# Reading the moving columns of four down-projections in other orders

## The chip, the core and the metric

The kernel runs on one core of a Trainium2 chip. The metric is the device time of one execution in microseconds; the time before is 997.28 us, the median of two runs. The engines are TensorE (PE, with its weight loads shown apart as PEld), VectorE (DVE), ScalarE (ACT), GpSimd (POOL) and SyncE (SP), which issues the DMAs. TensorE multiplies a stationary operand of 128 x 128 weights with a moving operand of up to 512 columns and adds the product into a bank of PSUM, its accumulator memory.

## The reference

The program is a decoder trunk of two layers over 256 tokens with 1024 features. Each layer is a half-step SwiGLU feed-forward network, a token mixer (stick-breaking attention in layer 0, a gated linear recurrence in layer 1), and another half-step feed-forward network. Each sub-layer normalises its input and is modulated by a conditioning vector. What matters here is the feed-forward network, of which there are four:

```python
def swiglu(h, w_gu, w_down):
    g, u = jnp.split(h @ w_gu, 2, axis=-1)
    return (jax.nn.silu(g) * u) @ w_down
...
    x = x + MACARON_W * g * swiglu(h, ffn_w_gu[layer, 0], ffn_w_down[layer, 0])
```

`w_down` has 2816 rows and 1024 columns. The product with it is the down-projection; its result is scaled by a gate and added to x.

## The kernel before

All activations lie with features on the 128 partitions and the 256 tokens along the columns. x is eight tiles of 128 x 256 (`xall`, lines 436 and 437), and the hidden layer of a feed-forward network is 22 such tiles. Sub-layers are named by a pair: (0,0), (0,2), (1,0) and (1,2) are the four feed-forward networks, (0,1) the attention, (1,1) the recurrence.

Every float32 number is split into a high part and a remainder, both kept as `float32r`, which TensorE takes in one pass. A product is then three matmuls into the same columns of a bank: high by high, high by remainder, remainder by high. `Acc.group` (lines 514 to 532) issues these three, all at line 526; `o`, `wc` and `xc` are functions that cut the columns of the bank, of the weights and of the moving operand:

```python
                seq = ((wh, xh), (wh, xl), (wl, xh))
                for n, i in enumerate(passes):
                    u, v = seq[i]
                    pe.matmul(o(b()), wc(u()), xc(v()), ...
```

Products with few uses are left whole and take TensorE's own float32 passes (`group32`, line 538, with its matmul at line 543: two k tiles of the recurrence's output projection, 16 matmuls). The attention's product of weights and values (line 951) and its running sums (lines 929 and 931) also call the matmul directly. In `values` the last three of each six matmuls read their moving operand as two runs of 128 columns, 384 apart, and write two runs of 128 columns, 256 apart.

`down` (from line 643) does a down-projection. The eight output tiles d lie in five banks, two to a bank but for the last two; bank halves are taken by `place`. For each k tile of the hidden layer and each d, `step(d, k)` calls `group` with the 256 columns of the hidden tile as moving operand and 256 consecutive columns of the bank as output. All but the last two chunks of weights run in the order of k; the last four k tiles run by d, so that the first output tiles are done early. Then `residual(d)` adds gate times bank to x[d] in one DVE instruction (line 666), and ACT and DVE make from x[d] the square for the next norm (`add_square`, line 601 for the sum) and the scaled tile that the next sub-layer's first products take before its norm is known (`scaled`, line 626). After the last sub-layer a sum of squares, a reciprocal root and six multiplications (line 1124) with their output DMAs end the program.

Weights arrive by DMA in pieces of 2048 columns, and `load` (from line 482) splits them on ACT (line 497) and DVE (line 500). Rows of the modulation weights are multiplied on DVE (line 564) between feed-forward tiles.

The order of all instructions is set in advance by a list scheduler (`Program.schedule`) from prices for each operation. `V(fn, T, ...)` gives a DVE operation its price by its number of columns, whatever instructions `fn` then issues, and a matmul group has a price by its columns alone. Each engine runs its own list in order, and waits for others on semaphores.

Of the kernel before, what the change touches and what calls it, by code (L numbers as in the profile page):

```python
# [44 lines left out]
NPAR = OFF_LAM + NR  # L45
NP0 = OFF_MB + 3 * KD  # what the first sub-layer needs

# [12 lines left out]

# [1 line left out]
class Space:  # L62
    """Memory that buffers take turns in, in program order: equal slots or an arena of cells."""

# [41 lines left out]
class Program:  # L106
# [58 lines left out]
    def schedule(self):  # L165
        ops = self.ops
        for o in ops:
            for d, data in o.deps.items():
                d.succ.append((o, data))
        # a buffer's users hold up whoever needs its place next  # L170
        spaces = {b.space for o in ops for b in o.bufs if b.space is not None}
# [33 lines left out]
        busy, gap, loads = 0.0, None, self.loads  # L205
        late = 0.0  # how far TensorE is behind its own time
        queue = {e: sorted((o for o in ops if o.eng == e), key=lambda o: (o.prio, o.seq)) for e in ("ACT", "DVE")}
# [4 lines left out]
        def guess(o, depth):  # L212
            """when an operation might start, from its inputs alone"""
            t = 0.0
            for d, data in o.deps.items():
                if d.start is not None:
                    t = max(t, d.end + self.lag(d, o, data))
                elif depth == 0:
                    return None
                else:  # L220
                    g = guess(d, depth - 1)
                    if g is None:
                        return None
                    t = max(t, max(g, free[d.eng]) + d.cost + self.lag(d, o, data))
            return t

        def wait_for(e, t, o):
            """an urgent operation, soon ready, that a start of o at t would hold up"""
            q = queue[e]
            while head[e] < len(q) and q[head[e]].start is not None:  # L230
                head[e] += 1
            n, i = 0, head[e]
            slack = o.prio + late - t
            while n < LOOK and i < len(q):
                u = q[i]
                i += 1
                if u.start is not None:
                    continue
                n += 1
                if u is o or u.prio >= o.prio:  # L240
                    break
                g = guess(u, 3)
                if g is None or g >= t + o.cost or g <= t:
                    continue
                if u.prio + late - g < o.cost and u.prio + late - g < slack - MARGIN:
                    return g
            return None
# [17 lines left out]
        while len(order) < len(ops):  # L265
# [60 lines left out]
            for b in o.bufs:  # L326
                b.uses -= 1
                if b.uses == 0 and b.space is not None:
                    sp = b.space
                    sp.live -= 1  # L330
                    # in-order engines: earlier readers on other engines have ended by their own time
                    t = o.end + 120.0 if b.hist else o.end
                    b.rel = max(getattr(b, "rel", 0.0), t)
                    for i in range(b.at, b.at + b.n):
                        sp.free[i] = b.rel
                    sp.last = max(sp.last, b.rel)
                else:
                    b.rel = max(getattr(b, "rel", 0.0), o.end + 120.0)
# [26 lines left out]
def trunk(ctx, tc, xT, cb, par, modw, gu0, gu, wdn, qk, wv, wo, win, wri, wout, out):  # L365
# [10 lines left out]

# [1 line left out]
    def ring(name, n, cols, dt=F32, pl=const):  # L378
# [52 lines left out]

# [1 line left out]
    def fixed(name, cols, dt=F32):  # L433
# [35 lines left out]

# [1 line left out]
    def dma(dst, src, n, w, after=(), lat=None):  # L471
# [10 lines left out]
    def load(src, n, name, chain=None, size=HALF):  # L482
        """n columns of weights: returns pieces of size columns, each (hi, lo)."""
        raw = Buf(rawr, name=f"raw_{name}")
# [22 lines left out]
    class Acc:  # L507
        """regions of one PSUM bank, with one start flag for the bank"""

# [4 lines left out]
        def group(self, part, o, w, wc, xs, xc, stop, parts=(None,), passes=(0, 1, 2)):  # L514
            """o += w[:, wc].T @ xs[:, xc] in three exact products"""
            b = self.b
# [21 lines left out]
    def group32(acc, part, o, w, wc, x32, xc, n, stop):  # L538
        """the same product, by TensorE's own float32 passes"""
        b = acc.b  # L540
# [8 lines left out]

# [1 line left out]
    mraw, mfin = {}, {}  # L551

    def mod_tile(l, s, w, t, after=(), lat=None):
        """row tile t of mod_w[l] for sub-layer s, part w (0 shift, 1 scale, 2 gate)."""
        key = (l, s, w)
# [12 lines left out]
    def mod_final(l, s, w, t0=0, n=KD):  # L568
# [4 lines left out]
        pp = [(pars, 0)] if l == s == 0 else [pars]  # L573
        mi = lambda: m()[:, t0 : t0 + n]  # noqa: E731
        fo = lambda: f()[:, t0 : t0 + n]  # noqa: E731
        if w == 0:
# [9 lines left out]

# [1 line left out]
    ssq, hcur, gcur = {}, {}, {}  # L588
# [27 lines left out]
    def scaled(gen, d):  # L616
        """x * scale and, in two more columns, the shift: what the first tile works on before the norm is known"""
        gs, sh = mfin[gen + (1,)], mfin[gen + (0,)]
        hi, lo = Buf(hxr), Buf(hxr)
        gcur.setdefault(gen, []).append((hi, lo))  # L620
        c = slice(d, d + 1)
        shc = lambda: sh()[:, c].to_broadcast([P, 2])  # noqa: E731
        A(lambda: hi()[:, T:], shc, AF.Copy, 2, [(sh, d)], [(hi, 1)])
# [19 lines left out]
    def down(l, s, nxt, srcs, ys, nlast, hook=None, post=None, n32=0):  # L643
        """x += gate * (W.T y) and what the next norm needs; srcs: chunks of two k tiles [P, 2, D];
        ys(k): (hi, lo), or one float32 tile for the first n32 chunks, and its columns."""
        accs = [Acc(f"acc_{l}_{s}_{i}") for i in range(5)]
# [5 lines left out]
        def step(d, k):  # L652
            acc, j = place[d]
            y, yc = ys(k)
            o = lambda b: b[:, j * T : (j + 1) * T]  # noqa: E731
            if k < 2 * n32:
                c0 = (k % 2) * D + d * P
                group32(acc, j, o, ws[k], lambda u: u[:, c0 : c0 + P], y, lambda v: v[:, yc], T, False)
            else:
                group(acc, j, o, ws[k], lambda u: u[:, d * P : (d + 1) * P], y, lambda v: v[:, yc], T, k == 2 * n - 1)  # L660

        def residual(d):
            acc, j = place[d]

            def fn():
                dve.scalar_tensor_tensor(x[d](), acc.b()[:, j * T : (j + 1) * T], gate()[:, d : d + 1], x[d](), ALU.mult,  # L666
                                         ALU.add)
            V(fn, T, [(acc.b, j), (gate, d), x[d]], [x[d]], ptr=1)
# [28 lines left out]
    def up(acc, ws, hx_):  # L697
        """acc = two regions of T columns: pieces of w [k, 2 P] against h"""
        for k in range(KD):
# [5 lines left out]
    def up_first(gen, ws, scale=(1.0, 1.0)):  # L705
        """the same products for the first tiles, on x * scale and shift: for each tile and region
        (tile, normed), column to add, its dependency"""
        gx = gcur.pop(gen)
# [20 lines left out]

# [1 line left out]
    def swiglu_tile(acc, y):  # L731
# [73 lines left out]

# [1 line left out]
    def attention(l, s, nxt, hook):  # L807
        R, F = new_phase(88, 24)
        # softplus(-lambda) for the recurrent block, with the same tables
        A(lam, lambda: col(OFF_LAM, NR), AF.Abs, NR, [pars], [lam], after=[pr.last_pe])  # L810
# [68 lines left out]

        W2 = 2 * S  # for each of two heads: block 0 (t = 0..255), block 1 (t = 128..255)  # L880
        BL = (slice(0, T), slice(T, S))
# [7 lines left out]
        def scores(f):  # L889
            """rows are keys s, columns queries t"""  # L890
            qh, ql = qs.pop(f)
# [49 lines left out]
        def values(f):  # L941
# [13 lines left out]
            for e in range(2):  # L955
                rows = slice(e * 64, (e + 1) * 64)
                bi = lambda e=e, rows=rows: b()[rows, e * T : (e + 1) * T]  # noqa: E731
                A(lambda rows=rows: oh()[rows, :], bi, AF.Copy, T, [b], [(oh, e)], psum=True)
# [29 lines left out]

# [1 line left out]
    def rglru(l, s, nxt):  # L990
        N32 = 1  # chunks of w_out that float32 passes take
        R, F = new_phase(8 * (NB - N32), 86)
# [137 lines left out]

# [1 line left out]
    last = []  # L1132
# [73 lines left out]

# [1 line left out]
    order = pr.schedule()  # L1208
# [58 lines left out]
```

## Time and profile before

| | |
|---|---|
| Runs | 997.07 and 997.49 us, median 997.28 |
| Profiled execution | span 994.6 us from the first to the last instruction; no time of its own is listed |
| Time outside the span | 2.7 us, from the median |
| TensorE | 980.2 us busy, 8096 matmuls |
| VectorE | 798.5 us busy |
| ScalarE | 561.8 us busy |
| DMA | 251.24 MB, 253 GB/s on average |

The span is the stretch from the first to the last instruction of one profiled execution. The page cuts it in 40 slices and shows each engine's busy share in tenths, and the clock that TensorE was granted. A line of the groups gives the kernel's line, the engine, the operation, out<-in, the shape and the count, then the busy time in us and the mean of one in ns, and then the idle time of the engine before them with what ended it. A line of the chain gives the start and the length in us of a piece of the chain of work that ended last, and how many instructions it has. The ends of matmuls are modelled, so the duration of one, some 280 ns, says little; the distance from one start to the next is what counts.

### The profile page before, as it was taken

The page shows a single profiled execution, that of the slowest core. Times are in us where ns is not written, and L with a number is a line of the kernel's source. Part 1 is how long each engine was busy: PE and PEld are TensorE (multiplying, and loading weights), DVE is VectorE, ACT ScalarE, POOL GpSimd, SP SyncE. Part 2 cuts the span into 40 slices and gives each one's busy share as a digit, 9 for nine tenths or more (in the row PEclk, how much of TensorE's full clock was granted, in tenths as well). Part 3 has the DMA queues.
Part 4 walks back from the last instruction along what each step waited for, and adds up shares of the span by engine and source line. Part 5 has one row for each costly group of instructions (what it writes and reads, how often), then busy time and mean ns, then how long its engine had stood idle before and what let it go on. Part 6 is the DMA issues. An engine that isn't in the chain of part 4 may idle for free.

```text
span 994.6 us, 19696 instructions
## 1 busy us (share of the span) xinstructions
PE 980.2 (99%) x8096; PEld 969.1 (97%) x8096; DVE 798.5 (80%) x1316; ACT 561.8 (56%) x902; POOL 2.2 (0%) x14
## 2 busy tenths in 40 slices
PE   7999999999999999999999999999999999999997
PEld 5999999999999999999999999999999999999996
DVE  7997887898988999888789989874997996555433
ACT  5475443379776854444366544443779785444333
POOL 0000000000000000000000000000000000000000
PEclk9999999999999999999999999999999999999999
DMA  9988898845666389899866988886334645545421
GB/s 341 358 317 316 326 331 304 338 166 193 241 232 234 143 307 334 328 343 336 313 266 254 333 326 334 335 308 214 107 134 163 254 176 210 205 174 191 165 111 43
DMA packets 48331, 251.24 MB, mean 253 GB/s; under 512 B 5489, under 2 KB 6129, under 8 KB 28530
## 3 DMA queue, kind: packets, MB, share of 16 engines
q1 hardware_dynamic: 48242, 249.99, 68.0%
q8 instruction: 63, 1.03, 0.4%
q14 instruction: 26, 0.21, 0.1%
HBM read 248.92 MB, written 1.05 MB: 251 GB/s over the span
## 4 chain that ended last, share of the span: by engine, by line
PE 98%; DVE 1%; DMA 0%; issue 0%; ACT 0%; SPq 0%; DVEq 0%
PE bank L526 90%; PE bank L836 2%; PE bank L902 1%; PE bank L1025 1%; PE bank L951 1%; PE bank L543 1%; PE bank L929 1%; DMA x<-in_xT 0%; PE bank L905 0%; PE bank L608 0%; PE bank L931 0%; DVE x L1124 0%; DVE ssq L1151 0%; DVE rawm L564 0%; DVEq L1262 0%
## 5 line engine op out<-in xcount | busy, mean ns | idle before, releaser
L526 PE MATMUL bank<-hx,wh 128*128 128x256 f32 (+1 forms) x3392 | 606.9, 282 | 2.5 <-ACT hx L476 2.5
L497 ACT ACTIVATE wh<-raw 128x1024 fp32r<-128x1024 f32 (+1 forms) x328 | 337.2, 1046 | 339.2 <-PE bank L526 238.3
L526 PEld LDWEIGHTS bank<-hx,wh 128*128 128x128 f32 x3392 | 520.7, 189 | 4.1 <-ACT hx L476 3.3
L500 DVE TENSOR_TENSOR wl<-raw,wh 128x1024 fp32r<-128x1024 f32 (+1 forms) x328 | 390.1, 1209 | 129.4 <-ACT wh L497 126.0
L526 PE MATMUL bank<-hx,wl 128*128 128x256 f32 (+1 forms) x1696 | 475.3, 280 | 0.0
L526 PEld LDWEIGHTS bank<-hx,wl 128*128 128x128 f32 x1696 | 320.5, 189 | 0.0
L526 PE MATMUL bank<-arenar,wh 128*128 128x256 f32 x1664 | 294.7, 280 | 0.0
L526 PEld LDWEIGHTS bank<-arenar,wh 128*128 128x128 f32 x1664 | 254.1, 188 | 0.1
L526 PE MATMUL bank<-arenar,wl 128*128 128x256 f32 x832 | 232.4, 279 | 0.0
L564 DVE SCALAR_TENSOR_TENSOR rawm<-rawm,cact 128x1024 f32<-128x1024 f32 x144 | 174.8, 1219 | 19.7 <-DMA rawm<-in_modw 19.3
L526 PEld LDWEIGHTS bank<-arenar,wl 128*128 128x128 f32 x832 | 156.1, 188 | 0.0
L476 ACT ACTIVATE arenar<-a 128x256 fp32r<-128x256 f32 x88 | 35.3, 404 | 4.4 <-DVE a L735 4.4
L740 DVE TENSOR_TENSOR arenar<-a,arenar 128x256 fp32r<-128x256 f32 x88 | 36.4, 418 | 0.5 <-ACT arenar L476 0.5
L735 DVE TENSOR_TENSOR a<-bank,sg 128x256 f32<-128x256 f32 x82 | 34.1, 418 | 0.1
L476 ACT ACTIVATE sg<-bank 128x256 f32<-128x256 f32 x82 | 30.2, 368 | 6.4 <-PE bank L526 4.8
L476 ACT ACTIVATE hx<-hpre,mf 128x256 fp32r<-128x256 f32 x48 | 23.3, 501 | 16.5 <-DVE mf L577 11.1
L666 DVE SCALAR_TENSOR_TENSOR x<-bank,mf,x 128x256 f32<-128x256 f32 x48 | 21.7, 478 | 11.2 <-PE bank L526 10.8
L476 ACT ACTIVATE hx<-x,mf 128x256 fp32r<-128x256 f32 x40 | 19.0, 502 | 18.2 <-DVE x L666 18.2
L636 DVE SCALAR_TENSOR_TENSOR hx<-hpre,mf,hx 128x256 fp32r<-128x256 f32 x48 | 22.7, 479 | 2.1 <-ACT hx L476 2.1
L836 PE MATMUL bank<-wh,hx 128*128 128x256 f32 x128 | 23.7, 282 | 0.0
L476 ACT ACTIVATE arenaf<-arenaf 128x768 f32<-128x768 f32 (+1 forms) x31 | 22.0, 737 | 0.5
L634 DVE SCALAR_TENSOR_TENSOR hpre<-x,mf,rst 128x256 f32<-128x256 f32 x48 | 21.6, 479 | 0.6 <-ACT rst L476 0.4
(97 smaller groups left out, 467.7 us busy)
## 6 DMA issues: line engine op xcount, KB each, us to landing
raw<-in_gu SPq DMA_DIRECT2D x79, 1024.0 KB, 5.2
rawm<-in_modw SPq DMA_DIRECT2D x144, 512.0 KB, 6.0
raw<-in_wdn SPq DMA_DIRECT2D x44, 1024.0 KB, 4.8
raw<-in_win SPq DMA_DIRECT2D x10, 1024.0 KB, 4.8
raw<-in_qk SPq DMA_DIRECT2D x8, 1024.0 KB, 5.3
raw<-in_gu SPq DMA_DIRECT2D x14, 512.0 KB, 6.0
raw<-in_wout SPq DMA_DIRECT2D x5, 1024.0 KB, 4.9
raw<-in_wv SPq DMA_DIRECT2D x4, 1024.0 KB, 7.0
```

The lines of the kernel that those rows point to most:

```text
L476: act.activation(o(), i(), f, **{k: (v() if callable(v) else v) for k, v in kw.items()})
L497: act.activation(h()[:, :m], raw()[:, a : a + m], AF.Copy)
L500: dve.tensor_tensor(lo()[:, :m], raw()[:, a : a + m], f32(h()[:, :m]), ALU.subtract)
L526: pe.matmul(o(b()), wc(u()), xc(v()), start=start and n == 0, stop=stop and n == len(passes) - 1, skip_group_check=True)
L543: pr.op("PE", c_mm(n, 4), lambda: pe.matmul(o(b()), wc(w()), xc(x32()), start=start, stop=stop, skip_group_check=True), [w, x32] + ([] if ...
L564: dve.scalar_tensor_tensor(raw(), raw(), 1.0, cact(), ALU.mult, ALU.mult, accum_out=m()[:, t : t + 1])
L634: V(lambda: dve.scalar_tensor_tensor(hp(), x[d](), gs()[:, c], q(), ALU.mult, ALU.mult), T, [x[d], (gs, d), q], [hp], ptr=1)
L636: V(lambda: dve.scalar_tensor_tensor(lo()[:, :T], hp(), sh()[:, c], f32(hi()[:, :T]), ALU.add, ALU.subtract), T, [hp, (sh, d), hi], [lo], ...
L666: dve.scalar_tensor_tensor(x[d](), acc.b()[:, j * T : (j + 1) * T], gate()[:, d : d + 1], x[d](), ALU.mult, ALU.add)
L735: V(lambda: dve.tensor_tensor(a(), b()[:, T:], sg(), ALU.mult), T, [(b, (1, 0)), sg], [a])
L740: V(lambda: dve.tensor_tensor(y[1](), a(), f32(y[0]()), ALU.subtract), n, [a, y[0]], [y[1]])
L836: pe.matmul(o, u()[:, tb * P : (tb + 1) * P], v()[:, c0 : c0 + 256], start=start and n == 0, stop=k == KD - 1 and n == 2, skip_group_check ...
```

## The change

The 256 columns of a tile are the tokens. A matmul's result does not depend on the order in which the columns pass, as long as each result is put back under its token. The change names two families of orders. `blocks(n, h)` cuts the columns in h equal parts and takes runs of n columns from the parts in turn. `halves(n)` takes every second run of n columns first and then the others.

- In (0,0) the order goes round eight patterns with the k tile (k modulo 8), and the bank is written in the same pattern as the hidden tile is read. So tokens land where they were, and nothing else changes. The first of the eight patterns is the plain order.
- In (0,2) the hidden tile is read by `blocks(16, 2)`, in (1,0) by `halves(16)` and in (1,2) by `blocks(2, 2)`. The bank is written in plain order, so it holds the tokens permuted. The residual add puts them back: it becomes two DVE instructions of 128 columns each, which walk the bank and x in matching patterns.

Attention and recurrence use the plain order in `down` as before, and `group32` gets `o` in plain order. Comments are taken out elsewhere in the file, which moves no line of code to another order.

```diff
+    def blocks(n, h):
+        return lambda ap: ap.rearrange("p (h c e) -> p c h e", h=h, e=n)
+    def halves(n):
+        return lambda ap: ap.rearrange("p (c h e) -> p h c e", h=2, e=n)
+    plain = lambda ap: ap
+    MIRRORED = (plain, blocks(16, 2), blocks(8, 2), blocks(4, 2), blocks(2, 2), blocks(16, 4), halves(16), halves(4))
+    ORDERS = {(0, 2): (blocks(16, 2), lambda ap: ap.rearrange("p (c h e) -> p h c e", h=2, e=16)),
+              (1, 0): (halves(16), lambda ap: ap.rearrange("p (h c e) -> p c h e", h=2, e=16)),
+              (1, 2): (blocks(2, 2), lambda ap: ap.rearrange("p (c h e) -> p h c e", h=2, e=2))}
...
-            o = lambda b: b[:, j * T : (j + 1) * T]  # noqa: E731
+            if (l, s) == (0, 0):
+                yo = wo_ = MIRRORED[k % len(MIRRORED)]
+            else:
+                yo, wo_ = ORDERS.get((l, s), (plain, plain))[0], plain
+            o = lambda b: wo_(b[:, j * T : (j + 1) * T])
...
-                group(acc, j, o, ws[k], lambda u: u[:, d * P : (d + 1) * P], y, lambda v: v[:, yc], T, k == 2 * n - 1)
+                group(acc, j, o, ws[k], lambda u: u[:, d * P : (d + 1) * P], y, lambda v: yo(v[:, yc]), T, k == 2 * n - 1)
...
-                dve.scalar_tensor_tensor(x[d](), acc.b()[:, j * T : (j + 1) * T], gate()[:, d : d + 1], x[d](), ALU.mult,
-                                         ALU.add)
+                i, t = acc.b()[:, j * T : (j + 1) * T], x[d]()
+                parts = [(t, i)]
+                if (l, s) in ORDERS:
+                    i = ORDERS[l, s][1](i)
+                    if (l, s) == (1, 0):
+                        t = t.rearrange("p (c h e) -> p c h e", h=2, e=16)
+                        parts = [(t[:, :, h, :], i[:, :, h, :]) for h in range(2)]
+                    else:
+                        t = t.rearrange("p (h c e) -> p h c e", h=2, e=i.shape[3])
+                        parts = [(t[:, h], i[:, h]) for h in range(2)]
+                for t, i in parts:
+                    dve.scalar_tensor_tensor(t, i, gate()[:, d : d + 1], t, ALU.mult, ALU.add)
```

## The prediction

> **What bounds the kernel now.** I read the page first, then the chain of work that ended last in order of time, then the windows of the four stages that the change touches.
>
> ```profile
> span 994.6 us, 19696 instructions
> PE 980.2 (99%) x8096; PEld 969.1 (97%) x8096; DVE 798.5 (80%) x1316; ACT 561.8 (56%) x902; POOL 2.2 (0%) x14
> ...
> PEclk9999999999999999999999999999999999999999
> ...
> PE 98%; DVE 1%; DMA 0%; issue 0%; ACT 0%; SPq 0%; DVEq 0%
> ```
>
> TensorE is busy 99% of the span, the granted clock is in its top tenth in all 40 slices, and 98% of the chain is matmuls. A busy TensorE alone would prove little, because the ends of matmuls are modelled. The chain is better evidence, for it counts starts.
>
> ```profile
> 334.35 186.94 PE bank L526 x1584
> 521.29 0.43 PE bank L608 x2
> 521.73 186.93 PE bank L526 x1584
> ...
> 804.67 181.19 PE bank L526 x1536
> 985.89 0.49 DVE x L666
> ```
>
> 186.94 us over 1584 matmuls is 118.0 ns from one start to the next, 186.93 over 1584 is the same, and 181.19 over 1536 is 118.0 again. Each piece runs through a whole feed-forward layer and into the next sub-layer without a break. A nanosecond more on a matmul of these stretches is therefore a nanosecond more on the time, and no wait stands by to absorb it. The down-projections are the last third of each feed-forward layer:
>
> ```profile
> 140.10:202.30 62.20, 62.20 (x531) 62.20 (x530) 1.00 0.87 325
> 453.30:515.50 62.20, 62.20 (x530) 62.20 (x529) 1.00 0.86 324
> 640.70:702.90 62.20, 62.20 (x531) 62.20 (x530) 1.00 0.69 250
> 923.50:985.85 62.35, 62.35 (x530) 62.14 (x528) 1.00 0.29 102
> ```
>
> The columns are the stretch, its length, TensorE's matmuls and its weight loads (busy time and count), the granted clock, the DMA share and GB/s. In the order of the code these are (0,0), (0,2), (1,0) and (1,2): 22 k tiles x 8 output tiles x 3 products = 528 matmuls each. 528 x 118.0 ns is 62.3 us, the length of each window. All four are matmuls and nothing else, at clock 1.00.
>
> **What sets 118 ns.** Whether another order of the columns costs anything depends on what paces a matmul today. Other rows have other widths:
>
> ```profile
> 236.53 0.88 PE L951 MATMUL bank<-arenar 128*128 128x512 f32 x3
> 237.24 0.52 PE L951 MATMUL bank<-arenar 128*128 128x256 f32 x3
> 237.60 0.52 PE L929 MATMUL bank<-arenar,ntri 128*128 128x384 f32 x2
> ...
> 237.77 0.36 PE bank L929 x2
> ...
> 768.97 6.91 PE bank L543 x32
> ```
>
> The first three rows are the timeline of one stretch of the attention, the others the chain. From 236.53 to 237.24 three matmuls of 512 columns start, 237 ns each; from 237.24 to 237.60 three of 256, 120 ns each; two of 384 take 0.36, 180 ns each. That is 0.46 to 0.47 ns a column at each width, so the pace is one of streaming columns, not of a weight load or a fixed cost per instruction: those would weigh less on 512 columns than on 256. L543 is the ordinary float32 product, which the trace shows as two records for each of its 16 matmuls; 6.91 us over 32 is 216 ns for a record. [...]
>
> **The change, part by part.**
>
> Changed matmuls. In (0,0) three of the 22 k tiles keep the plain order (k = 0, 8, 16), and 19 x 24 = 456 matmuls read and write in a changed order. The other three layers change the reading only, 528 each. Together that is 2040 of 8096. No matmul is added.
>
> Price of a changed matmul. The row at 237.24 is the nearest from below: those three matmuls (L951, second half) read their moving operand as two runs of 128 and write two runs of 128. At 120 ns they show that a pattern with one jump costs 2 ns at most, on the reading and the writing side. From above the nearest row is L543: 256 columns in 216 ns, +98 ns. [...] Every price between nothing and +98 ns is open, and it can differ by run length:
>
> - Runs of 16 and 8 (15 to 31 jumps a matmul): all of (0,2) and (1,0), and k mod 8 = 1, 2, 5, 6 of (0,0). A run is still many columns; I take the row with one jump, nothing.
> - Runs of 4: k mod 8 = 3 and 7 of (0,0), 5 x 24 = 120 matmuls. I take nothing; at the upper end it would be 120 x 98 ns = 11.8 us.
> - Runs of 2: all of (1,2), 528, and k = 4, 12, 20 of (0,0), 72, together 600. Here 127 of 255 steps jump 512 bytes. [...] So I take the upper row: 600 x 98 ns = 58.8 us. Exactly half pace, +118 ns, would be 70.8 us; one column slot of 0.46 ns per jump, 58 ns, would be 35 us.
>
> [...]
>
> Residual adds. In (0,2), (1,0) and (1,2) each of the eight adds at L666 becomes two over 128 columns, 24 more DVE instructions.
>
> ```profile
> L666 DVE SCALAR_TENSOR_TENSOR x<-bank,mf,x 128x256 f32<-128x256 f32 x48 | 21.7, 478 | 11.2 <-PE bank L526 10.8
> L723 DVE SCALAR_TENSOR_TENSOR tr<-bank,rst 128x256 f32<-128x256 f32 x20 | 8.3, 417 | 0.0
> L1082 DVE SCALAR_TENSOR_TENSOR arenaf<-arenaf 128x512 f32<-128x512 f32 x5 | 3.1, 685 | 4.6 <-ACT arenaf L476 4.6
> ...
> 504.00:515.60 11.60, 11.60 (x100) 11.60 (x100) 9.83 (x21) 7.38 (x15) 0.00 (x0) 1.00 0.75 292
> 515.60:527.00 11.40, 11.40 (x96) 11.35 (x95) 10.85 (x19) 10.59 (x17) 0.00 (x0) 1.00 0.50 185
> ```
>
> (685 - 417) / 256 is 1.05 ns a column, so half of L666 is 478 - 134 = 344 ns, and two in a row at most 688: +0.21 us an add, 5.0 us of DVE time in all. I assume that the order in which VectorE walks bank and x costs it nothing; twice the column price would make it +0.48 us. At the handover from (0,2) to (1,0), the two windows quoted, DVE has 1.8 and 0.6 us left (third busy figure: 9.83 of 11.60 and 10.85 of 11.40), against 8 x 0.21 = 1.7 us of additions; the one after (1,0) is alike. What would be late next are the scaled tiles for the next sub-layer, queued behind these adds, and weight remainders. The next sub-layer's first tile takes its eight input tiles in turn, 6 matmuls or 0.7 us each, so the last of them is needed some 5 us after the first, and that hides a lag of 1.7 us. If that cover were gone, it would cost about 1 us a handover. At the very end nothing hides the last add, which the chain shows at 985.89: +0.2 us.
>
> Everything else, the DMAs, the weight splitting and the order of operations, has the same prices in the planner and does not move.
>
> Sum: 994.6 + 58.8 + 0.2 = 1053.6 us of span. The median of the two runs, 997.28, is 2.7 above the span, which lies outside the first and last instruction. So 997.28 + 59.0 = **1056.3 us**, +5.9%.
>
> **The rivals.**
>
> (1) *No order costs anything.* For it: the two-run row, and the plain possibility that a fetch gives just two columns. [...] Time: 997.28 + 0.2 = 997.5, with handover lags up to 1000. [...]
>
> (2) *Scattered writes into the bank cost, reads don't.* Only (0,0) writes scattered: 456 x 98 ns = 44.7 us, 1042. Against it, again the row at 237.24, with its two runs in the bank. [...]
>
> (3) *Both* the short runs and the scattered writes cost: 528 + 456 = 984 matmuls x 98 ns = 96.4 us, 1094.
>
> (4) *Every jump pattern falls to the slow pace:* 2040 x 98 ns = 199.9 us, 1197. The two-run row speaks against it.
>
> [...]
>
> **How the numbers follow.** The forecast has 0.36, rival 1 0.30, rival 2 0.13, rival 3 0.08, rival 4 0.09, rival 5 0.04. The forecast's own range, from 58 ns to 118 ns for runs of 2, is 1032 to 1069. With rivals 1 and 2 that leaves 0.21 out, so the range takes in rival 3: 996 to 1095. Two per cent, 20 us, is about what a measurement of this kernel tells from no change. Slower by more: the forecast and rivals 2 to 4, 0.66. Within: rival 1 and a weak form of rival 5, 0.31. Faster: 0.03.
>
> **What would show it.** In the profile after, the window of (1,2) should grow from 62 to about 114 us at clock 1.00, (0,2) and (1,0) should stay at 62, and (0,0) at about 69, with its starts 216 ns apart only at k = 4, 12 and 20. [...] If (0,0) grows by 45 us, it is the bank. L666 should show 72 instructions where it had 48, and the gap between the last matmul and the final square should grow by about 0.2 us. [...]

## The result, and the profile after

The changed kernel takes 1035.78 us (1035.09 and 1036.46), against 997.28 before. The ratio is 1.0381, with a 95% interval from 1.0365 to 1.0398: slower by 38.5 us.

On the page of the changed kernel, the span, the busy times and the clock answer to the lines quoted of before:

```profile
span 1033.4 us, 19720 instructions
PE 1017.7 (98%) x8096; PEld 1005.9 (97%) x8096; DVE 802.0 (78%) x1340; ACT 562.9 (54%) x902; POOL 2.2 (0%) x14
...
PEclk9999999999999999999999999999999999999999
...
PE 98%; DMA 1%; DVE 0%; issue 0%; SPq 0%; ACT 0%; DVEq 0%
```

The number of matmuls is the same, the clock is the same, 24 DVE instructions have come, and TensorE is busy 37.5 us longer. It is still 98% of the chain. The windows of the four down-projections say where, from the first start of each to the first start after it (length, TensorE and weight loads with their counts, clock, DMA share, GB/s; a count takes in two or three matmuls that reach over the edge):

```profile
141.88:209.25 67.37, 67.37 (x530) 67.37 (x529) 1.00 0.83 304
460.16:523.52 63.36, 63.36 (x530) 63.36 (x529) 1.00 0.88 320
648.69:712.06 63.37, 63.37 (x531) 63.37 (x529) 1.00 0.68 246
932.80:1024.31 91.51, 91.51 (x530) 91.37 (x528) 1.00 0.20 69
```

Each holds 528 starts. Before, the same stretch was 62.2 us, 117.8 ns a matmul. Now (0,0) has 127.6 ns, (0,2) and (1,0) 120.0, and (1,2), the one in runs of 2, 173.3. The growth is 5.2 + 1.2 + 1.2 + 29.3 = 36.9 us of the 38.8 by which the spans differ. The chain, start and length in us, shows where the rest lies:

```profile
2.97 7.28 DMA rawm<-in_modw
...
14.33 200.83 PE bank L526 x1632
...
341.32 188.12 PE bank L526 x1584
...
813.97 210.52 PE bank L526 x1536
1024.52 0.62 DVE x L698 x2
1025.16 0.42 ACT sq L476
```

The first long stretch begins at 14.33 instead of 13.05, after a DMA of modulation weights, and its up-projection takes 127.55 us (14.33 to 141.88) instead of 127.05. Both come before anything that the change touches. In the seven runs below that leave everything up to the first down-projection as it was, the first start fell between 13.2 and 14.3 us, and that up-projection took 127.1 to 128.0. So these 1.8 us are scatter and no part of the change. The stretch of 188.12 was 186.94: it grew by 1.18, the 1.2 of its down-projection, so the handover into the next sub-layer lost nothing. At the end the two adds take 0.64 us to the square, where one took 0.52.

### The profile page after: what moved, and what is told of

Same layout as the page of the kernel before. It is cut to its first block, busy times and chain, and to the rows that moved or that the text cites. A ratio compares the mean times of both kernels' runs of the same rounds, so it can differ in the third digit from the quotient of the medians.

```text
span 1033.4 us, 19720 instructions
## 1 busy us (share of the span) xinstructions
PE 1017.7 (98%) x8096; PEld 1005.9 (97%) x8096; DVE 802.0 (78%) x1340; ACT 562.9 (54%) x902; POOL 2.2 (0%) x14
## 4 chain that ended last, share of the span: by engine, by line
PE 98%; DMA 1%; DVE 0%; issue 0%; SPq 0%; ACT 0%; DVEq 0%
PE bank L526 91%; PE bank L867 2%; PE bank L933 1%; PE bank L1056 1%; PE bank L982 1%; DMA rawm<-in_modw 1%; PE bank L543 1%; PE bank L960 1%; PE bank L936 0%; PE bank L625 0%; PE bank L962 0%; DVE x L1155 0%; SPq L472 0%; DVE rawm L564 0%; DVE x L698 0%
## 5 line engine op out<-in xcount | busy, mean ns | idle before, releaser
L497 ACT ACTIVATE wh<-raw 128x1024 fp32r<-128x1024 f32 (+1 forms) x328 | 337.3, 1046 | 370.0 <-PE bank L526 262.3
L500 DVE TENSOR_TENSOR wl<-raw,wh 128x1024 fp32r<-128x1024 f32 (+1 forms) x328 | 390.2, 1210 | 160.2 <-ACT wh L497 156.9
L526 PE MATMUL bank<-arenar,wh 128*128 128x256 f32 x1664 | 331.1, 297 | 0.0
L526 PEld LDWEIGHTS bank<-arenar,wh 128*128 128x128 f32 x1664 | 269.6, 191 | 0.1
L526 PE MATMUL bank<-arenar,wl 128*128 128x256 f32 x832 | 247.5, 297 | 0.0
L526 PEld LDWEIGHTS bank<-arenar,wl 128*128 128x128 f32 x832 | 159.1, 191 | 0.0
L698 DVE SCALAR_TENSOR_TENSOR x<-bank,mf,x 128x128 f32<-128x128 f32 (+1 forms) x72 | 24.8, 390 | 20.1 <-PE bank L526 19.9
```

Of the source, the lines that this page charges most:

```text
L497: act.activation(h()[:, :m], raw()[:, a : a + m], AF.Copy)
L500: dve.tensor_tensor(lo()[:, :m], raw()[:, a : a + m], f32(h()[:, :m]), ALU.subtract)
L526: pe.matmul(o(b()), wc(u()), xc(v()), start=start and n == 0, stop=stop and n == len(passes) - 1, skip_group_check=True)
L698: dve.scalar_tensor_tensor(t, i, gate()[:, d : d + 1], t, ALU.mult, ALU.add)
```

## The experiments

From here on a piece is four consecutive columns, the first at a multiple of four. The theory at the start, F: TensorE's moving columns come in such pieces, and a piece that is used in part has to be fetched again. The size of a piece and the fetching are my assumptions; what the runs below measure is a step in price between every second run of 4 (117.0 ns a matmul) and every second run of 2 (226.6). The rivals: J, each jump costs a slot, whatever its kind; D, only alternating between two places 512 bytes apart collides; and rival 2 of the prediction, that scattered writing into the bank costs.

**One part taken back: (1,2) in plain order, with whole adds.**

```diff
-              (1, 0): (halves(16), ...),
-              (1, 2): (blocks(2, 2), ...)}
+              (1, 0): (halves(16), ...)}
```

> The changed kernel with sub-layer (1,2) in plain order again. If the short runs carry most of the cost, its window goes from 91.5 us back to 62.2 and the time from 1035.8 to about 1006.5 us; what stays over the 997.3 of before is 5.2 us in (0,0), 1.2 in (0,2), 1.2 in (1,0) and about 1.5 that no matmul of a down-projection explains. If something else in the change (the split adds, a shift at the start) held it up, the time stays over 1010.

It takes 1004.82 us, a ratio of 1.0074 (1.0057 to 1.0091). The last window of this run is back where it was, the first as in the changed kernel:

```profile
142.35:209.73 67.38, 67.38 (x531) 67.38 (x529) 1.00 0.83 306
...
933.90:996.09 62.19, 62.19 (x530) 62.15 (x528) 1.00 0.30 102
```

So (1,2) carries 1035.8 - 1004.8 = 31 us of the 38.5 by the medians and 29.3 by its window, and the remaining 7.6 us over the 997.25 of before in this comparison are the 5.2 + 1.2 + 1.2 of the other three. The 1.5 us that the expectation added for what no window explained do not show in the median; the four runs lie between 1004.48 and 1006.81, so a difference of that size is within their scatter.

**Reading alone, four run lengths.** From here on the experiments start from the kernel before, with whole adds, and a table gives each sub-layer an order for reading. `blocks` takes runs from several places in turn, which I call alternating.

```diff
-                group(acc, j, o, ws[k], ..., y, lambda v: v[:, yc], T, k == 2 * n - 1)
+                group(acc, j, o, ws[k], ..., y, lambda v: yo(v[:, yc]), T, k == 2 * n - 1)
...
+    READ = {(0, 0): blocks(1, 2), (0, 2): blocks(4, 2), (1, 0): blocks(8, 2), (1, 2): blocks(2, 2)}
```

> Reading alone is reordered, in runs of 1, 4, 8 and 2 (in (0,0), (0,2), (1,0), (1,2)), always alternating between the two halves of the tile; tokens aren't put back, so results stand under other tokens, and the adds are whole. Theory F (the feed fetches aligned pieces of four columns, and a piece that is used in part has to be fetched again; 128 fetches in the 173.3 ns of runs of 2, 1.35 ns each): runs of 1 need 256 fetches, 347 ns a matmul; runs of 4 and 8 need no more pieces than plain, 118 to 126. Theory J (each jump costs a slot, 55.5 ns over 127 jumps, 0.44 ns): runs of 1 take 229, runs of 4 145, runs of 8 131. Theory D (alternating between two places 512 bytes apart collides): as J here. All expect 173 for runs of 2.

The windows, in the order of the table:

```profile
141.28:200.24 58.96, 58.96 (x530) 58.96 (x529) 1.00 0.89 329
452.71:519.59 66.88, 66.88 (x531) 66.88 (x529) 1.00 0.83 303
644.75:709.87 65.12, 65.12 (x530) 65.12 (x529) 1.00 0.66 240
930.62:1022.13 91.51, 91.51 (x530) 91.37 (x528) 1.00 0.20 69
```

Over 528 these are 111.7 ns for runs of 1, 126.7 for runs of 4, 123.3 for runs of 8 and 173.3 for runs of 2. The last is the price in the changed kernel to the digit, so it is one of reading. J falls, as 63 jumps cost 9 ns and not 27 (runs of 4). And runs of 1, which all three theories made the worst, are **quicker than plain order**, by 6.1 ns. F as I had put it falls too.

**Stepping instead of alternating.** The same run lengths by `halves`: every second run, then the others.

```diff
+    READ = {(0, 0): halves(1), (0, 2): halves(4), (1, 0): halves(8), (1, 2): halves(2)}
```

> Reading alone, every second run first and then the others, in runs of 1, 4, 8 and 2 (in (0,0), (0,2), (1,0), (1,2)); tokens aren't put back. The order steps forward through the tile twice and never alternates between places far apart. Theory F: runs of 1 use two columns of each piece on each way, so 128 fetches, 173 ns; runs of 2 the same 173; runs of 4 and 8 use whole pieces, 118. Theory J: runs of 2 173, runs of 4 145, runs of 8 131. Theory D: 118 for all four, since nothing alternates.

The windows of the four down-projections, in the same order:

```profile
140.42:261.84 121.42, 121.42 (x530) 109.72 (x529) 1.00 0.46 169
512.78:574.58 61.80, 61.80 (x531) 61.80 (x529) 1.00 0.90 325
699.73:761.33 61.60, 61.60 (x530) 61.60 (x529) 1.00 0.69 253
982.06:1101.73 119.67, 119.67 (x530) 109.07 (x528) 1.00 0.16 53
```

Every second column costs 230.0 ns, every second run of 2 costs 226.6, where F had 173 for both. Runs of 4 and 8 are free, 117.0 and 116.7; the runs of 16 that (1,0) of the changed kernel reads in the same way took 120.0. Nothing alternates here, so D falls: two columns used of each piece of four is expensive without any jump back. Twice 117.8 is 235.6, so these two orders go at about half pace, 1.8 ns for each of the 128 visits that they pay to pieces.

**The same piece again.** Here orders repeat columns by a zero step.

```diff
+    READ = {(0, 0): one_piece, (0, 2): half_twice, (1, 0): blocks(2, 16), (1, 2): one_column}
```

> Orders that repeat columns, so a part of the product is left out and another part counted several times. (0,0) reads the first four columns 64 times; (0,2) reads the first half of each piece of four twice, then goes on to the next piece; (1,0) reads runs of 2 from 16 places 64 bytes apart in turn; (1,2) reads one column 256 times. Theory F: (0,2) visits 64 pieces in order, 118 ns, though it has 127 jumps; (1,0) 173. [...] Theory J: (0,2) 173, (0,0) 145, (1,0) 173. Theory D: (0,2) 118, (1,0) somewhere between 118 and 173. [...]

The four windows:

```profile
141.16:200.12 58.96, 58.96 (x531) 58.96 (x529) 1.00 0.87 317
454.15:516.34 62.19, 62.19 (x530) 62.19 (x529) 1.00 0.87 326
641.52:757.66 116.14, 116.14 (x530) 108.75 (x529) 1.00 0.37 134
978.43:1037.39 58.96, 58.96 (x530) 58.94 (x528) 1.00 0.32 108
```

The second row is the one that tells theories apart: it reads only half of each piece, twice, with as many jumps as runs of 2, and takes 117.8, the plain price. So it is not the jumps that cost, and going on to another piece is what is left. That can't be the whole rule, because runs of 1 from two halves go to another piece at every column and take 111.7. The third row, runs of 2 from 16 places, takes 220.0, more than any theory had. The first and last rows stay in one piece and take 111.7, the same as the shuffled halves. So plain order takes 6.1 ns longer than an order that stays in one piece, and 111.7 is the lowest price in these runs; no run says what holds it there.

**Writing alone.**

```diff
+    WRITE = {(0, 0): blocks(2, 2), (0, 2): blocks(4, 2), (1, 0): halves(2), (1, 2): blocks(16, 2)}
```

> Reading is plain, and the bank is written in runs of 2, 4, and 16 from two halves and in every second run of 2 ((0,0), (0,2), (1,2); (1,0)); tokens aren't put back. My theory by now is that writing costs nothing and the whole price lies in reading: all four sub-layers 117.8 ns a matmul, 62.2 us a window, about 997 us in all. Rival 2 of the prediction, scattered writes at the pace of a float32 pass: 216 ns, 114 us a window, worst for runs of 2.

The windows of the two sub-layers that write in runs of 2:

```profile
140.42:202.61 62.19, 62.19 (x531) 62.19 (x529) 1.00 0.88 331
...
640.88:703.06 62.18, 62.18 (x530) 62.18 (x529) 1.00 0.70 250
```

All four windows are 62.2 us, and the run took 996.66. Runs of 2 in the bank, alternating or stepping, cost nothing; rival 2 falls. Runs of 1 were not tried for writing, and runs of 8 not by themselves. The changed (0,0) agrees: with the reading prices alone (120.0 for all runs of 16, of which `blocks(16, 4)` wasn't measured by itself) its 22 k tiles come to 67.6 us, against 67.4.

**Single columns from other places.** Why should shuffled halves be quick? Theory G by now: columns go in pairs, and the first and the second place of a pair each keep a piece at hand. H: the distance helps.

```diff
+    def pairs(c):
+        return lambda ap: ap.rearrange("p (g h c) -> p g c h", h=2, c=c)
+    READ = {(0, 0): blocks(1, 4), (0, 2): pairs(4), (1, 0): pairs(16), (1, 2): blocks(1, 16)}
```

> Reading alone, in runs of 1; tokens aren't put back. (0,0) takes columns from four quarters in turn, (0,2) shuffles the two halves of each 8 columns (0 4 1 5 2 6 3 7), (1,0) the two halves of each 32, (1,2) takes columns from 16 places in turn. Theory G: columns go in pairs, and the first and the second place of the pair each have a piece of four columns at hand; a pair whose places both stay in the piece they had is free, one that changes to another piece costs about 1.8 ns. Then (0,2) and (1,0) fall to 111.7 like the shuffle of the two halves of 256, since each place runs through its piece to the end; (0,0) alternates pieces in each place at every pair, 173 to 230; (1,2) 230. Rival theory H: it is the distance of 512 bytes that makes the shuffle of halves quick, two places in different parts of the memory that are fetched at once. Then (0,2), 16 bytes apart, is no quicker than plain, 118 or more, and (0,0), 256 bytes apart, need not be slow.

The four windows:

```profile
141.01:214.93 73.92, 73.92 (x531) 73.92 (x530) 1.00 0.76 279
465.84:524.80 58.96, 58.96 (x531) 58.96 (x530) 1.00 0.91 335
649.97:708.92 58.95, 58.95 (x530) 58.95 (x529) 1.00 0.71 264
929.66:1045.81 116.15, 116.15 (x530) 108.55 (x528) 1.00 0.16 55
```

Shuffling columns that lie 16 or 64 bytes apart brings 111.7 as well: H falls. Sixteen places cost 220.0, near the 230 of G. Four places cost 140.0, where G said 173 to 230. So G, with two places that each run through their own piece, fits the quick rows, but it has no account of a piece that is left and soon returned to.

**Alternating between more places.**

```diff
+    READ = {(0, 0): blocks(2, 4), (0, 2): blocks(2, 8), (1, 0): blocks(1, 8), (1, 2): blocks(4, 4)}
```

> Reading alone; tokens aren't put back. Runs of 2 from four places in turn (0,0) and from eight (0,2), runs of 1 from eight (1,0), runs of 4 from four (1,2). A piece of four columns that was left is returned to after three or seven other pieces, where runs of 2 from two places return after one (173 ns) and from sixteen after fifteen (220). Theory K: a left piece is kept for a short while, so that the return after one other piece is cheap and a later one pays again: 220 for runs of 2 from four and from eight, 220 for runs of 1 from eight. Rival theory L: the price is one of jumps, the same 127 at each count of places: 173 for both, and the 220 of sixteen places has to do with their distance of 64 bytes. Runs of 4 use each piece whole, so by both close to the 126.7 of runs of 4 from two places.

The four windows:

```profile
140.82:259.34 118.52, 118.52 (x530) 108.93 (x529) 1.00 0.47 174
510.27:631.67 121.40, 121.40 (x530) 109.28 (x529) 1.00 0.45 167
756.86:873.01 116.15, 116.15 (x531) 108.23 (x530) 1.00 0.38 134
1093.76:1165.33 71.57, 71.57 (x530) 71.50 (x528) 1.00 0.27 89
```

224.5 and 229.9 ns for runs of 2 from four and eight places, 220.0 for single columns from eight, and 135.5 for runs of 4 from four. L falls: with the same 127 jumps, two places cost 173 and four 225. K fits these rows: runs of 2 that return to a piece after one other cost 55.5 ns over plain order, later ones 107 to 112. It does not fit the 140.0 of single columns from four places, which return after three others, unless each place of a pair is counted for itself as in G; and then it has no account of why 140.0 and 173.3 differ. Whether and how long a piece is kept, and why whole pieces in alternation (126.7, 135.5) cost more than stepping ones (117.0), stays open.

**A version that uses the quick order.** The two halves of the moving tile are shuffled column by column wherever 256 columns are read in `up`, in the first tiles of (0,0) and in `down`. Hidden tiles stay shuffled, so the residual add undoes two shuffles in (0,0), (0,2), (1,0) and (1,2), and one elsewhere. It does so in one instruction, and the evictions of the other projections put tokens back too. Hidden tiles that come from a product of 258 columns, which stays in plain order, are shuffled when they are split.

```diff
+    def spread(ap):
+        return ap.rearrange("p (h c) -> p c h", h=2)
+    def back(ap, h):
+        return ap.rearrange("p (c h) -> p h c", h=h)
...
+                h = 2 if s == 1 else 4
+                t = rows(x[d](), h)
+                dve.scalar_tensor_tensor(t, back(acc.b()[:, j * T : (j + 1) * T], h), gate()[:, d : d + 1], t, ALU.mult,
+                                         ALU.add)
```

> The kernel before with 7104 of its matmuls reading the two halves of the moving tile in turn, column by column (1056 + 2880 in the up-projections, 2112 + 384 in the down-projections, 672 in the attention's and recurrence's input projections). The hidden tiles stay in the shuffled order; the residual adds and the evictions of the other projections put tokens back in one instruction each. If the 6.1 ns saved per matmul hold wherever they are used: 7104 x 6.1 ns = 43.3 us, 997.3 - 43.3 = 954 us. If ACT and DVE become late with strided reads and writes, or the weights do (117.8 us of splitting per 100 us don't get quicker), some of it is lost: 960 to 985. If the gain belongs to the down-projections alone: 997.3 - 2112 x 6.1 ns = 984.

It takes 964.42 us, a ratio of 0.9663 (0.9647 to 0.968): faster than the kernel before by 3.4%, and than the changed one by 6.9%. The profiled execution is the slowest of its four, 968.93 us. From the page, the chain by engine; then the window of (0,2), and three pieces of the chain in order of time:

```profile
PE 85%; DVE 7%; DMA 4%; ACT 2%; issue 1%; SPq 0%; DVEq 0%
```

```profile
441.42:500.38 58.96, 58.96 (x531) 58.96 (x529) 1.00 0.89 331
```

```profile
485.15 1.15 DVE wl L500
...
488.14 7.17 DMA rawm<-in_modw
...
748.71 10.19 PE bank L543 x32
```

The down-projections hold 111.7 ns. Of the 43.3 us worked out, 32.5 arrived (996.93 - 964.42). TensorE is now 85% of the chain and no longer 98%: at the start and at handovers the chain goes through split weights (L500) and modulation rows on VectorE, which had time to spare before (798.5 us busy of a span of 994.6). And the whole float32 products at L543 went from 6.91 to 10.19 us. The expectation's 117.8 us of splitting per 100 us is too much: in the kernel before, L500 is busy 390.1 us and L497 337.2 us of the span of 994.6, 73 per 100 together.

**The same with the recurrence's output projection in plain order.** The edit is against the version above; `group` takes `yo` in the same way, and the add of (1,1) walks bank and x plainly.

```diff
+            yo = (lambda ap: ap) if (l, s) == (1, 1) else spread
...
-                group32(acc, j, o, ws[k], ..., y, lambda v: spread(v[:, yc]), T, False)
+                group32(acc, j, o, ws[k], ..., y, lambda v: yo(v[:, yc]), T, False)
```

> The spread kernel with the recurrence's output projection read in plain order again: 16 whole float32 matmuls and 192 in three products. In the spread kernel the 32 records of the whole ones took 10.2 us where they took 6.9. If the shuffled order is what slows them, they go back to 6.9 and the 192 lose 192 x 6.1 ns = 1.2 us of gain: 964.4 - 3.3 + 1.2, some 962 us. If the 10.2 us were a wait of another kind, the time goes up to 966.

The whole float32 products in the chain of this version:

```profile
743.65 7.17 PE bank L543 x32
```

L543 is at 7.17, near the 6.91 of before, so the shuffled order is what slows a whole float32 product, from 216 (6.91 us over 32) to 318 ns a record. The time is 962.73 us, 0.9671 (0.9644 to 0.9697): the two versions can't be told apart.

## Why the prediction was right, and where it was off

- *What bounds the kernel.* Right. Every nanosecond on a matmul came out as time: the windows grew by 36.9 us and the span by 38.8, of which 1.8 lie ahead of the first down-projection.
- *What sets 118 ns.* Right in so far as it lies with the columns: the order of reading them alone moved the pace, down to 111.7 ns and up to 230.0. What holds plain order at 117.8 ns is not shown.
- *Runs of 16 and 8 cost nothing.* Nearly. Runs of 16 cost 2.2 ns, in all 2.3 us in (0,2) and (1,0), and runs of 8 from two halves 5.5 ns. The row with one jump was no sufficient bound for 15 of them.
- *Runs of 4 cost nothing.* Off by 9 ns in alternation; stepping, they are free.
- *Runs of 2 cost +98 ns.* This is the term that was mis-sized. That runs of 2 go at the pace of L543 was my estimate, and no run shows its 98 ns for the order used here; the runs showed 55.5 ns, 29.3 us in (1,2) where 528 x 98 ns makes 51.7. With the 72 matmuls in (0,0) at the same price, 4.0 us, it brought 33.3 us instead of 58.8. The runs of 4 to 16, which I put at nothing, brought 3.5 us, so the total came closer than its terms. The upper row that I took, 216 ns, is near by number for runs of 2 that do not return to a piece soon (226.6, 224.5, 229.9 ns), though nothing shows that they are slow for its reason. The order used here returns to a piece after one other, which costs 173.3. I named one column slot per jump as a lower end, 58 ns. It comes close by number and is wrong as a mechanism, since the orders with the same 127 jumps span 117.8 to 229.9.
- *The split adds.* The cost per half was 344 by the sum, and the profile has 345:

```profile
L698 DVE SCALAR_TENSOR_TENSOR x<-bank,mf,x 128x128 f32<-128x128 f32 x48 | 13.8, 345 | 16.9 <-PE bank L526 16.7
L698 DVE SCALAR_TENSOR_TENSOR x<-bank,mf,x 128x256 f32<-128x256 f32 x24 | 10.9, 480 | 3.3 <-PE bank L526 3.2
```

  So the order in which DVE walks bank and x, in runs of 2 or 16, costs nothing that shows. At the end the two halves overlap, +0.12 us instead of 0.21, and the handovers hide the others, as expected.
- *Time outside the span.* I had 2.7 us from a median and one span; the runs that list both have 1.7 to 1.9 (1035.09 - 1033.4 in the changed kernel). It cancels in the difference.
- *The rivals.* 1 rested in part on a fetch of two columns, which runs of 2 in steps rule out (226.6 ns). 2 and 3 fall with the run that only writes (62.2 us a window), 4 with the runs of 16 (120.0 ns). A faster kernel, the 0.04 of rival 5, did not come of the orders of this change, and yet plain order is not the quickest (117.8 against 111.7 ns), which is what the last version lives on.

## What to carry to other kernels

Where `float32r` products fill TensorE's time, look at how the moving operand's pattern visits the pieces of four columns. In these runs it was free to use each piece whole by taking every second run of 4 or 8 columns first, or its half twice in a row. Whole pieces in alternation, and every second run of 16, cost 2 to 18 ns a matmul. To leave each piece half used cost 102 to 112 ns, and 55.5 where the order returned after one other piece; runs of 2 were the worst of the orders in this change. Reading two half tiles in turn, column by column, gained 6 ns of 118 and cost no instruction (19696 in both kernels), because the results are evicted anyway, but only the `float32r` products gained: whole float32 products became slower, 318 ns a record instead of 216. Scattered writing into the bank, in runs of 2, 4 and 16, was free (62.2 us a window, as before).

## What was not expected

Single columns from two places (111.7 ns) are quicker than plain order (117.8), whether the places lie 16, 64 or 512 bytes apart, though this has the most jumps of all. Runs of 2 between the same two places are slow (173.3). The price is therefore not monotonic in run length: 111.7, 173.3, 126.7, 123.3 and 120.0 for 1, 2, 4, 8 and 16 between two halves. Pieces visited by the two places of a pair side by side would account for the quick and the free orders and for the full price of 220 to 230. They do not account for the 140.0 and 173.3 between, nor for the 120.0 to 135.5 of whole pieces in alternation, and no run shows the pairs themselves, so the mechanism stays open.
